# Two stages of each FFN's down-projection as seven products of quarters, with the weight sums made by accumulating DMAs

## The chip, the cores and the metric

The kernel runs on one core of one Trainium2 chip; the seven other cores are idle. The metric is the device time of one execution in microseconds, the median of three runs. TensorE (PE) multiplies, VectorE (DVE) and ScalarE (ACT) do the element-wise work, SyncE (SP) issues the loads, and GpSimd (POOL) sets a few small tiles.

## What is computed

Two layers on 512 tokens of 1024 features: in the first a retention mixer, in the second stick-breaking attention, each with a gated FFN behind it. The change is in the FFN:

```python
D_MODEL, SEQ, D_FF = 1024, 512, 2816
def _conv_ffn(h, w_up, conv_w, conv_b, w_down):
    u = h @ w_up                                  # [512, 2 * 2816]
    u = causal_depthwise_conv(u, conv_w) + conv_b # width 3
    gate, val = jnp.split(u, 2, axis=-1)
    return (jax.nn.silu(gate) * val) @ w_down     # [512, 2816] @ [2816, 1024]
x = x + _conv_ffn(_rmsnorm(x, g), ...)            # all in float32
```

## The kernel before

Activations lie feature-major, as tiles of 128 features by 512 tokens. The residual is eight such tiles, `self.x` (printed as x_72 to x_79 in the order of instructions). A float32 operand of a product is held as two float32r parts: `chunk` (L94) loads 128 x 1024 weights into a `raw` buffer (three of them, a DMA from SP, L101), ACT rounds them into `hi` (L102) and DVE takes the rest into `lo` (L103); there are four buffers of each. `split` (L79) does the same for activations. `mm3` (L106) makes each product of tiles out of three matmuls, hi by hi, hi by lo and lo by hi (L109 to L111).

`ffn` (L394) goes over 22 tiles f of the 2816 inner features. For each, `ffn_act` (L380) makes two up-projections of 24 matmuls (`up`, L367: scaling L374, convolution L375 and L377), the gate (L383, L384) and the split of the activation (L84, L85). `down` (L388) multiplies a stage of these tiles by its weights: layer 0 has stages of 8, 8 and 6 tiles, layer 1 stages of 8, 6 and 4, and its last four tiles belong to the final norm. The first two stages of a layer run in the middle of the loop over f, two tiles after the last one that they need. A stage goes over the eight output tiles m: one weight chunk of (k tiles x 128) columns, `proj` into one PSUM tile `att` (four buffers), and `add_to_x` (L160), one DVE addition of 512 columns to the residual (L161).

Every engine runs its own queue in order. A scheduler sets the order within each queue when the kernel is built; it puts the split of a chunk several chunks ahead of its matmuls, as far as the buffers reach.

Of the kernel before, what the change touches and what calls it, by code (L numbers as in the profile page):

```python
# [34 lines left out]
class Kernel:  # L35
    """Activations are kept feature-major ([128 features, 512 tokens] tiles), so every
    projection takes its operands as they lie. A float32 operand of a large product is held as
    hi + lo, each of 12 significant bits (float32r), and the product is hi*hi + lo*hi + hi*lo."""

    def __init__(self, ctx, tc, t):  # L40
# [20 lines left out]
    BUFS = {"xh": 8, "xl": 8, "qk": 8, "vv": 8, "yy": 16, "pp": 8, "tt": 8, "rr": 2, "cs": 4}  # L61

    def sb(self, tag, cols=S, dt=F32):
        return self.ap.tile([P, cols], dt, tag=tag, bufs=self.BUFS[tag], name=self.name(tag))

# [13 lines left out]
    def split(self, src, tag, cols=S, scale=None):  # L79
        """hi + lo = src (* scale, per partition), exactly."""  # L80
# [13 lines left out]
    def chunk(self, c, cols=CH):  # L94
        """Weight chunk c of the stream: [128, cols], as hi + lo."""
        nc = self.nc
        raw = self.raw()
        hi = self.wp.tile([P, CH], F32R, tag="hi", bufs=4, name=self.name("hi"))
        lo = self.wp.tile([P, CH], F32R, tag="lo", bufs=4, name=self.name("lo"))
        raw, hi, lo = raw[:, :cols], hi[:, :cols], lo[:, :cols]  # L100
        nc.sync.dma_start(raw, c)  # L101
# [4 lines left out]
    def mm3(self, out, a, b, start, stop):  # L106
        """out (+)= a.T @ b for a, b given as (hi, lo)."""
# [26 lines left out]
    def proj(self, w, xs, out=None):  # L134
        """Feature-major projection by one [nk x 128, 128] chunk of weights."""
# [11 lines left out]
    def out_proj_steps(self, name, base, ys, last):  # L147
        """XT += W.T @ y over the k tiles of ys; chunks hold [k tiles, 256 columns]."""
# [555 lines left out]
```

## Time and profile before

| | us |
|---|---|
| median of 3 runs | 1389.34 (1389.16 to 1389.47) |
| span of the profiled execution | 1387.6 |
| PE busy | 1375.7 (99%) |
| DVE busy | 940.1 (68%) |
| ACT busy | 592.6 (43%) |
| POOL busy | 6.8 (0%) |

The profiled execution is shown by its span, first to last instruction; the runs' time is 1.7 us more than it, and holds what lies before and after. Matmuls are pipelined, so a busy PE says only that some matmul was under way; how fast they follow each other is read from their starts. A group's line gives count, busy time, mean duration, and the idle time of its engine just before it with what ended that. A stretch of time (a window) gives busy time by engine and the granted TensorE clock, where 1.00 is 2.4 GHz and 0.50 is 1.2 GHz.

### The profile page before, as it was taken

How to read it: one execution, taken by the hardware profiler on the slowest of the kernel's cores; microseconds unless marked ns; L12 is line 12 of the kernel's file. 1: busy time of each engine (PE TensorE's matmuls, PEld its weight loads, DVE VectorE, ACT ScalarE, POOL GpSimd, SP SyncE). 2: the span in 40 equal slices, each digit the busy share in tenths (PEclk: the TensorE clock that was granted, in tenths of full speed). 3: DMA queues.
4: the chain of work that ended last, by engine and by line, in shares of the span. 5: the costliest groups of instructions: out<-in, count | busy, mean ns of one | idle time of the engine just before them, and what ended most of it. 6: DMA issues, size and time to landing. Idle time of an engine off the chain costs nothing.

```text
span 1387.6 us, 17028 instructions
## 1 busy us (share of the span) xinstructions
PE 1375.7 (99%) x6668; PEld 1140.9 (82%) x6668; DVE 940.1 (68%) x1282; ACT 592.6 (43%) x867; POOL 6.8 (0%) x69
## 2 busy tenths in 40 slices
PE   9999999999999999999999999999999999999997
PEld 7888888888888888888888888787788888888887
DVE  7774564654669773676367779889788753765765
ACT  5443332433355441443244655554355432433434
POOL 0000000000000000000000000000000000000000
PEclk9999999999999999999999999999999999999999
DMA  8233133131324333233322431120133233223221
GB/s 266 72 93 105 56 106 107 50 102 61 91 84 127 94 93 105 92 98 100 91 84 69 122 92 52 57 72 25 56 105 123 92 94 103 84 86 120 72 95 62
DMA packets 41025, 126.88 MB, mean 91 GB/s; under 512 B 4592, under 2 KB 6768, under 8 KB 40944
## 3 DMA queue, kind: packets, MB, share of 16 engines
q1 hardware_dynamic: 39424, 124.45, 29.0%
q10 hardware_dynamic: 1520, 1.33, 0.3%
q8 instruction: 53, 0.87, 0.3%
q14 instruction: 28, 0.23, 0.1%
HBM read 123.67 MB, written 2.10 MB: 91 GB/s over the span
## 4 chain that ended last, share of the span: by engine, by line
PE 96%; DVE 3%; ACT 0%; issue 0%; DMA 0%; DVEq 0%; ACTq 0%
PE acc L109 22%; PE acc L111 22%; PE acc L110 22%; PE att L109 8%; PE att L110 8%; PE att L111 8%; PE one L484 2%; PE z L458 1%; PE tp L476 1%; DVE cs L464 1%; DVE lo L103 1%; DVE tt L430 0%; DVE tt L427 0%; PE one L188 0%; PE one L223 0%
## 5 line engine op out<-in xcount | busy, mean ns | idle before, releaser
L102 ACT CAST hi<-raw 128x1024 fp32r<-128x1024 f32 (+2 forms) x253 | 244.6, 968 | 389.2 <-PE acc L110 182.0
L110 PE MATMUL acc<-xl,hi 128*128 128x512 f32 x960 | 374.6, 390 | 0.0
L111 PE MATMUL acc<-xh,lo 128*128 128x512 f32 x960 | 374.2, 390 | 0.0
L109 PE MATMUL acc<-xh,hi 128*128 128x512 f32 x960 | 374.2, 390 | 0.0
L103 DVE TENSOR_TENSOR lo<-raw,hi 128x1024 fp32r<-128x1024 f32 (+2 forms) x253 | 281.9, 1115 | 46.6 <-ACT hi L102 38.0
L111 PEld LDWEIGHTS acc<-xh,lo 128*128 128x128 f32 x960 | 180.2, 188 | 38.0 <-issue 0.5
L109 PEld LDWEIGHTS acc<-xh,hi 128*128 128x128 f32 x960 | 180.2, 188 | 36.6 <-issue 0.5
L110 PEld LDWEIGHTS acc<-xl,hi 128*128 128x128 f32 x960 | 180.3, 188 | 36.0
L377 DVE SCALAR_TENSOR_TENSOR tt<-tt,vec,tt 128x511 f32<-128x511 f32 (+1 forms) x176 | 131.2, 747 | 4.0 <-ACT tt L375 1.1
L374 DVE TENSOR_TENSOR tt<-acc,rr 128x512 f32<-128x512 f32 x80 | 55.0, 687 | 85.5 <-PE acc L111 85.5
L161 DVE TENSOR_TENSOR x<-x,att 128x512 f32<-128x512 f32 x40 | 27.4, 686 | 91.8 <-PE att L111 91.8
L109 PE MATMUL acc<-yy,hi 128*128 128x512 f32 x224 | 87.7, 392 | 0.1
L110 PE MATMUL acc<-yy,hi 128*128 128x512 f32 x224 | 87.6, 391 | 0.0
L111 PE MATMUL acc<-yy,lo 128*128 128x512 f32 x224 | 87.5, 391 | 0.0
L111 PE MATMUL acc<-hi,xl 128*128 128x512 f32 (+1 forms) x256 | 86.0, 336 | 0.0
L110 PE MATMUL acc<-lo,xh 128*128 128x512 f32 (+1 forms) x256 | 85.9, 336 | 0.0
L109 PE MATMUL acc<-hi,xh 128*128 128x512 f32 (+1 forms) x256 | 85.9, 336 | 0.0
L375 ACT ACTIVATE tt<-tt,vec 128x512 f32<-128x512 f32 x88 | 71.6, 814 | 7.5 <-DVE tt L374 6.4
L161 DVE TENSOR_TENSOR x<-x,acc 128x512 f32<-128x512 f32 x64 | 43.3, 684 | 43.2 <-PE acc L111 43.0
L111 PE MATMUL att<-yy,lo 128*128 128x512 f32 (+1 forms) x176 | 65.1, 370 | 0.0
L109 PE MATMUL att<-yy,hi 128*128 128x512 f32 (+1 forms) x176 | 65.1, 370 | 0.0
L110 PE MATMUL att<-yy,hi 128*128 128x512 f32 (+1 forms) x176 | 65.1, 370 | 0.0
(162 smaller groups left out, 1958.6 us busy)
## 6 DMA issues: line engine op xcount, KB each, us to landing
raw<-in_up SPq DMA_DIRECT2D x80, 512.0 KB, 3.6
raw<-in_down SPq DMA_DIRECT2D x24, 512.0 KB, 3.6
raw<-in_rv SPq DMA_DIRECT2D x16, 512.0 KB, 3.9
raw<-in_rg SPq DMA_DIRECT2D x16, 512.0 KB, 3.7
raw<-in_rout SPq DMA_DIRECT2D x16, 512.0 KB, 3.6
raw<-in_rqk SPq DMA_DIRECT2D x12, 512.0 KB, 3.7
raw<-in_down SPq DMA_DIRECT2D x16, 384.0 KB, 3.0
raw<-in_sqk SPq DMA_DIRECT2D x12, 512.0 KB, 3.7
```

The lines of the kernel that those rows point to most:

```text
L102: nc.scalar.copy(hi, raw)
L103: nc.vector.tensor_sub(lo, raw, hi.bitcast(F32))
L109: mm(out, a[0], b[0], start=start, stop=False)
L110: mm(out, a[0], b[1], start=False, stop=False)
L111: mm(out, a[1], b[0], start=False, stop=stop)
L161: self.nc.vector.tensor_add(self.x[m], self.x[m], ps)
L374: nc.vector.tensor_mul(u, ps, self.r)
L375: nc.scalar.activation(c, u, AF.Identity, scale=w[2], bias=w[3])
L377: nc.vector.scalar_tensor_tensor(c[:, i:], u[:, : S - i], w[2 - i], c[:, i:], op0=ALU.mult, op1=ALU.add)
L458: nc.tensor.matmul(z[:, :nz], q[:, i * P : (i + 1) * P], k[:, :nz], start=m == 0, stop=m == 1)
L464: nc.vector.tensor_tensor_scan(left[:, :n][:, ::-1], sg[:, :n][:, ::-1], self.diag[:, S - n :][:, ::-1], 0.0, op0=ALU.mult, op1=ALU.max,)
L484: self.nc.tensor.matmul(o[e * DH : (e + 1) * DH, i * P : (i + 1) * P], v[p // 4 * NT + j][:, h * DH : (h + 1) * DH], aT[e][:, j * P : (j + ...
```

## The change

For the first two stages of each FFN (`FAST`), the product of weights and activations is taken as 2 x 2 blocks: even and odd k tiles, even and odd output tiles, first and second 256 tokens. Seven products of blocks, with sums and differences as operands, take the place of eight.

- **Activations.** Two tiles f are collected in one tile `ar` of 2048 columns. DVE forms the differences T3, T1 (one operation of 512 columns), T2 and T4 (256 each), and one split of 1792 columns holds all seven operands (`oh`, `ol`).
- **Weights.** A stage runs as two halves of four output tiles (`fast_down`). A half loads w21, w11, w12 and w22 plainly (SP) and makes four sums by DMAs from POOL that add into the tile: w22 onto w21 in `sums`, then w11, then w12 onto the same tile, and w21 onto w11 in `raw`. Each sum is split by ACT and DVE before the next one is added. `sums` has two buffers, `hi` and `lo` now have five.
- **Products.** In order: T1 into z, X11 into x, T2 onto x, X21 into y (an `acc` tile), T3 onto x, X22 onto z, T4 onto x. Each goes over two output tiles p, 3 x (k tiles / 2) matmuls of 256 columns for each, and is followed by two additions of 256 columns to the residual. x and z go on accumulating after they have been read.
- **Memory.** Some activation buffers live in a pool per phase (`phase`), so that FFN and mixers share the space; the third stage uses `acc` tiles.

```diff
+FAST = (2, 2)
+Q = S // 2
...
+    def phase(self, which):
+        if self.pp is not None:
+            self.pp.__exit__(None, None, None)
+            self.pp = None
+        if which:
+            self.pp = self.tc.tile_pool(name=self.name(which), bufs=1, reuse_waits="tile")
+            self.ph = self.pp.__enter__()
...
-    BUFS = {"xh": 8, "xl": 8, "qk": 8, "vv": 8, "yy": 16, "pp": 8, "tt": 8, "rr": 2, "cs": 4}
+    BUFS = {"xh": 8, "xl": 8, "tt": 8, "rr": 2}
+    PHASE = {"qk": 8, "vv": 8, "yy": 16, "pp": 8, "cs": 4, "ar": 2, "oh": 5, "ol": 5}
...
         raw = self.raw()
-        hi = self.wp.tile([P, CH], F32R, tag="hi", bufs=4, name=self.name("hi"))
-        lo = self.wp.tile([P, CH], F32R, tag="lo", bufs=4, name=self.name("lo"))
+        nc.sync.dma_start(raw[:, :cols], c)
+        return self.parts(raw, cols)
+    def parts(self, raw, cols=CH):
+        nc = self.nc
+        hi = self.wp.tile([P, CH], F32R, tag="hi", bufs=5, name=self.name("hi"))
+        lo = self.wp.tile([P, CH], F32R, tag="lo", bufs=5, name=self.name("lo"))
         raw, hi, lo = raw[:, :cols], hi[:, :cols], lo[:, :cols]
-        nc.sync.dma_start(raw, c)
         nc.scalar.copy(hi, raw)
...
+    T3, T1, T2, T4, X21, X22, X11 = range(7)
     def ffn_act(self, l, f, ps):
         nc = self.nc
         g, v = self.up(l, f, ps[0]), self.up(l, NF + f, ps[1])
         nc.scalar.activation(g, g, AF.Silu)
-        nc.vector.tensor_mul(v, g, v)
-        tag = ("yy", "yy", "vv", "qk")[f % 4]
-        return self.split(v, (tag, tag))
+        if f % 2 == 0:
+            self.pair = self.sb("ar", 8 * Q)
+        y = self.pair[:, 6 * Q :] if f % 2 == 0 else self.pair[:, 4 * Q : 6 * Q]
+        nc.vector.tensor_mul(y, g, v)
+        if f >= STAGES[l][FAST[l] - 1][1]:
+            if f % 2 == 0:
+                self.two = self.sb("oh", 7 * Q, F32R), self.sb("ol", 7 * Q, F32R)
+            hi, lo = [x[:, f % 2 * S : (f % 2 + 1) * S] for x in self.two]
+            nc.scalar.copy(hi, y)
+            nc.vector.tensor_sub(lo, y, hi.bitcast(F32))
+            return hi, lo
+        if f % 2 == 0:
+            return None
+        part = lambda i, n=1: self.pair[:, i * Q : (i + n) * Q]
+        two = lambda x: x.rearrange("p (a q) -> p a q", a=2)
+        x12 = part(7)
+        nc.vector.tensor_sub(two(part(self.T3, 2)), two(part(self.X22, 2)), x12[:, None].broadcast_to([P, 2, Q]))
+        nc.vector.scalar_tensor_tensor(part(self.T2), part(self.T1), -1.0, part(self.X22), op0=ALU.mult, op1=ALU.subtract)
+        nc.vector.scalar_tensor_tensor(part(self.T4), part(self.T2), -1.0, part(self.X21), op0=ALU.mult, op1=ALU.subtract)
+        hi, lo = self.sb("oh", 7 * Q, F32R), self.sb("ol", 7 * Q, F32R)
+        nc.scalar.copy(hi, part(0, 7))
+        nc.vector.tensor_sub(lo, part(0, 7), hi.bitcast(F32))
+        return hi, lo
     def down(self, l, a, s, last):
         lo, hi = STAGES[l][s]
         for m in range(KD):
             w = self.wchunk(f"down{l}_{s}", m, (hi - lo) * P)
-            self.add_to_x(m, self.proj(w, a[lo:hi], None if last is not None else self.att()), last)
+            self.add_to_x(m, self.proj(w, a[lo:hi]), last)
+    def quarter(self, out, w, p, ops, n, start):
+        mm, nk = self.nc.tensor.matmul, len(ops)
+        for k, op in enumerate(ops):
+            c, o = slice((nk * p + k) * P, (nk * p + k + 1) * P), slice(n * Q, (n + 1) * Q)
+            a, b = [x[:, c] for x in w], [x[:, o] for x in op]
+            for i, (ai, bi) in enumerate(((0, 0), (0, 1), (1, 0))):
+                mm(out[:, :Q], a[ai], b[bi], start=start and k + i == 0, stop=k == nk - 1 and i == 2,
+                   skip_group_check=not start)
+    def fast_down(self, l, s, ops, half):
+        nc, t = self.nc, self.t[f"fast{l}_{s}"][half]
+        cols = 2 * len(ops) * P
+        w11, w12, w21, w22 = t[0], t[1], t[2], t[3]
+        first, second = slice(0, Q), slice(Q, S)
+        x = [self.psum("x", 2) for _ in range(2)]
+        z = [self.psum("z", 2) for _ in range(2)]
+        sums = self.wp.tile([P, CH], F32, tag="sums", bufs=2, name=self.name("sums"))
+        raw = self.raw()
+        def load(to, w, add=False):
+            if add:
+                nc.gpsimd.dma_start(to[:, :cols], w, accum_op=ALU.add)
+            else:
+                nc.sync.dma_start(to[:, :cols], w)
+        def product(to, w, n, start=False):
+            for p in range(2):
+                self.quarter(to[p], w, p, ops, n, start)
+        def add(row, tokens, of, sign=1):
+            for p in range(2):
+                x = self.x[4 * half + 2 * p + row][:, tokens]
+                (nc.vector.tensor_add if sign > 0 else nc.vector.tensor_sub)(x, x, of[p][:, :Q])
+        load(sums, w21)
+        load(sums, w22, True)
+        load(raw, w11)
+        w = self.parts(sums, cols)
+        product(z, w, self.T1, True)
+        add(1, second, z, -1)
+        load(sums, w11, True)
+        w = self.parts(raw, cols)
+        product(x, w, self.X11, True)
+        add(0, first, x)
+        load(raw, w21, True)
+        w = self.parts(sums, cols)
+        product(x, w, self.T2)
+        add(0, second, x)
+        load(sums, w12, True)
+        w = self.chunk(w12, cols)
+        y = [self.acc() for _ in range(2)]
+        product(y, w, self.X21, True)
+        add(0, first, y)
+        w = self.parts(raw, cols)
+        product(x, w, self.T3)
+        add(1, second, x, -1)
+        w = self.parts(sums, cols)
+        product(z, w, self.X22)
+        add(0, second, z)
+        w = self.chunk(w22, cols)
+        product(x, w, self.T4)
+        add(1, first, x, -1)
     def ffn(self, l, last):
         a, s = [], 0
         first = self.first4(f"ufirst{l}")
+        self.phase("ffn")
         for f in range(NF):
             a.append(self.ffn_act(l, f, first[2 * f : 2 * f + 2] if f < 2 else (None, None)))
+            if f == 1:
+                self.swap_pool()
             if s < 2 and f == STAGES[l][s][1] + 1:
-                self.down(l, a, s, None)
+                lo, hi = STAGES[l][s]
+                for half in range(2):
+                    self.fast_down(l, s, a[lo + 1 : hi : 2], half)
                 s += 1
+        self.swap_pool()
         self.down(l, a, s, last)
+        self.phase("mix" if last is not None else None)
         return a
...
+def _quarters(w, nk):
+    w = w.reshape(nk, 2, P, 2, 2, 2, P)
+    return w.transpose(3, 5, 1, 2, 4, 0, 6).reshape(2, 4, P, 2 * nk * P)
...
-            a[f"down{l}_{s}"] = _rows(ffn_w_down[l][lo * P : hi * P], hi - lo, P)
+            w = ffn_w_down[l][lo * P : hi * P]
+            if s < FAST[l]:
+                a[f"fast{l}_{s}"] = _quarters(w, (hi - lo) // 2)
+            else:
+                a[f"down{l}_{s}"] = _rows(w, hi - lo, P)
...
-    nc = _bacc.Bacc("TRN2", target_bir_lowering=False, num_devices=1)
+    nc = _bacc.Bacc("TRN2", target_bir_lowering=False, num_devices=1, dynamic_dma_scratch_size=1024)
```

What the change does to the queues, first on DVE in layer 0's first stage. Before, splits of weights (lo) and additions to the residual take turns; att is the PSUM tile of one output tile:

```order
L161 TENSOR_TENSOR x_74<-x_74,att_4028 128x512
L103 TENSOR_TENSOR lo_4152<-raw_4150,hi_4151 128x1024
L161 TENSOR_TENSOR x_75<-x_75,att_4060 128x512
L103 TENSOR_TENSOR lo_4184<-raw_4182,hi_4183 128x1024
L161 TENSOR_TENSOR x_76<-x_76,att_4092 128x512
L103 TENSOR_TENSOR lo_4216<-raw_4214,hi_4215 128x1024
L161 TENSOR_TENSOR x_77<-x_77,att_4124 128x512
L103 TENSOR_TENSOR lo_4253<-raw_4251,hi_4252 128x1024
```

After, the second half of the same stage: z, x and acc are PSUM tiles of 256 columns, x_75 to x_82 now the residual, sums_4201 and raw_4202 the two weight tiles that DMAs add into. The rows begin with the additions of the sixth product:

```order
L480 TENSOR_TENSOR x_77<-x_77,z_3972 128x256
L130 TENSOR_TENSOR lo_4269<-sums_4201,hi_4268 128x1024
L480 TENSOR_TENSOR x_76<-x_76,x_3969 128x256
L130 TENSOR_TENSOR lo_4302<-raw_4299,hi_4301 128x1024
L480 TENSOR_TENSOR x_78<-x_78,x_3970 128x256
L130 TENSOR_TENSOR lo_4334<-raw_4202,hi_4333 128x1024
L480 TENSOR_TENSOR x_80<-x_80,z_4199 128x256
L480 TENSOR_TENSOR x_82<-x_82,z_4200 128x256
L130 TENSOR_TENSOR lo_4364<-sums_4201,hi_4363 128x1024
L480 TENSOR_TENSOR x_79<-x_79,x_4197 128x256
L480 TENSOR_TENSOR x_81<-x_81,x_4198 128x256
```

The split of the sums for product 13 (lo_4364) now stands ahead of the additions of product 9 (x_79 and x_81 from x), and that for product 10 (lo_4269) behind the additions of product 6.

On POOL, before, the queue goes from its set-up straight to the small tiles of the attention (cs):

```order
L225 ISA
L225 AFFINE_SELECT diag<-diag 128x128
L463 MEMSET cs_6034 128x1
L463 MEMSET cs_6082 128x1
L463 MEMSET cs_6125 128x1
```

After, 32 DMAs stand there; these are the nine of layer 0's first stage and of the next stage's first sum (sums_5068):

```order
L469 DMA sums_3973<-in_fast_0 128x1024
L469 DMA sums_4201<-in_fast_0 128x1024
L469 DMA sums_3973<-in_fast_0 128x1024
L469 DMA raw_3974<-in_fast_0 128x1024
L469 DMA sums_3973<-in_fast_0 128x1024
L469 DMA sums_5068<-in_fast_1 128x1024
L469 DMA sums_4201<-in_fast_0 128x1024
L469 DMA raw_4202<-in_fast_0 128x1024
L469 DMA sums_4201<-in_fast_0 128x1024
```

A DMA into sums_4201 stands behind the first one of the next stage, and the three into it follow one another.

At the same stage's start, on DVE, before (tt, yy: the last activation and its split; att_3964: the stage's first output tile):

```order
L377 SCALAR_TENSOR_TENSOR tt_3947<-tt_3946,vec,tt_3947 128x511
L377 SCALAR_TENSOR_TENSOR tt_3947<-tt_3946,vec,tt_3947 128x510
L384 TENSOR_TENSOR tt_3947<-tt_3910,tt_3947 128x512
L85 TENSOR_TENSOR yy_3955<-tt_3947,yy_3954 128x512
L161 TENSOR_TENSOR x_72<-x_72,att_3964 128x512
L103 TENSOR_TENSOR lo_4088<-raw_4086,hi_4087 128x1024
L161 TENSOR_TENSOR x_73<-x_73,att_3996 128x512
L103 TENSOR_TENSOR lo_4120<-raw_4118,hi_4119 128x1024
```

After, where ar is the pair of activations and z and x are the tiles of products 1 to 3 of the first half:

```order
L404 SCALAR_TENSOR_TENSOR tt_3955<-tt_3954,vec,tt_3955 128x510
L480 TENSOR_TENSOR x_78<-x_78,z_3972 128x256
L418 TENSOR_TENSOR ar_3884<-tt_3918,tt_3955 128x512
L480 TENSOR_TENSOR x_75<-x_75,x_3969 128x256
L431 TENSOR_TENSOR ar_3884<-ar_3884 128x512
L130 TENSOR_TENSOR lo_4136<-sums_3973,hi_4135 128x1024
L432 SCALAR_TENSOR_TENSOR ar_3884<-ar_3884 128x256
L480 TENSOR_TENSOR x_77<-x_77,x_3970 128x256
L433 SCALAR_TENSOR_TENSOR ar_3884<-ar_3884 128x256
L480 TENSOR_TENSOR x_75<-x_75,x_3969 128x256
L130 TENSOR_TENSOR lo_4168<-raw_4165,hi_4167 128x1024
```

The additions of products 1 to 3 now stand among the last activations' differences (ar) and the split for product 6 (lo_4136).

## Rows read from the trace of the kernel before

**Rows 1.** The page: busy time by engine, and the chain that ended last.

```profile
PE 1375.7 (99%) x6668; PEld 1140.9 (82%) x6668; DVE 940.1 (68%) x1282; ACT 592.6 (43%) x867; POOL 6.8 (0%) x69
PE 96%; DVE 3%; ACT 0%; issue 0%; DMA 0%; DVEq 0%; ACTq 0%
```

**Rows 2.** Stretches (columns in the first line): the four stages, then an up-projection.

```profile
core 0: us, PE busy (x) PEld busy (x) DVE busy (x) ACT busy (x) POOL busy (x), PEclk, DMA share, GB/s
511.20:554.70 43.50, 43.50 (x193) 36.04 (x192) 18.00 (x20) 9.77 (x11) 0.00 (x0) 1.00 0.31 97
641.80:685.30 43.50, 43.50 (x194) 36.02 (x193) 18.00 (x20) 9.76 (x11) 0.00 (x0) 1.00 0.32 97
1124.50:1168.00 43.50, 43.50 (x194) 36.03 (x192) 18.00 (x20) 9.77 (x11) 0.00 (x0) 1.00 0.31 98
1233.30:1265.90 32.60, 32.60 (x145) 27.02 (x144) 16.52 (x20) 8.68 (x11) 0.00 (x0) 1.00 0.38 110
446.00:489.50 43.50, 43.50 (x194) 36.02 (x193) 31.75 (x40) 19.67 (x26) 0.00 (x0) 1.00 0.32 98
```

**Rows 3.** PE in time: start us, length us, engine, line, operation.

```profile
1339.58 0.39 PE L110 MATMUL att<-vv,hi 128*128 128x512 f32 x1
...
1352.73 0.39 PE L111 MATMUL att<-yy,lo 128*128 128x512 f32 x1
1352.96 0.28 PE L109 MATMUL att<-vv,hi 128*128 128x256 f32 x1
...
1364.47 0.28 PE L109 MATMUL att<-vv,hi 128*128 128x256 f32 x1
```

**Rows 4.** Groups by shape on DVE: count, then busy us, mean ns, idle before.

```profile
L103 DVE TENSOR_TENSOR lo<-raw,hi 128x1024 fp32r<-128x1024 f32 x193 | 235.6, 1221 | 31.3 <-ACT hi L102 26.7 <-PE att L110 1.5
L377 DVE SCALAR_TENSOR_TENSOR tt<-tt,vec,tt 128x511 f32<-128x511 f32 x88 | 65.6, 745 | 1.3 <-ACT tt L375 1.1
L103 DVE TENSOR_TENSOR lo<-raw,hi 128x512 fp32r<-128x512 f32 x40 | 27.3, 685 | 15.4 <-ACT hi L102 11.3 <-PE one L188 4.1
L103 DVE TENSOR_TENSOR lo<-raw,hi 128x768 fp32r<-128x768 f32 x20 | 19.1, 954 | 0.0
L568 DVE TENSOR_TENSOR x<-x,att 128x256 f32<-128x256 f32 x16 | 6.7, 417 | 6.1 <-PE att L111 5.6
```

**Rows 5.** Groups by shape on ACT: the splits' first halves.

```profile
L102 ACT CAST hi<-raw 128x1024 fp32r<-128x1024 f32 x193 | 203.2, 1053 | 319.6 <-PE acc L110 157.8 <-PE att L110 121.6 <-issue 17.5
L102 ACT CAST hi<-raw 128x768 fp32r<-128x768 f32 x20 | 16.8, 839 | 24.7 <-PE acc L110 10.7 <-PE att L110 9.2 <-ACT pp L461 2.8
```

**Rows 6.** DVE and ACT in time, at the first stage's start.

```profile
511.18 1.05 ACT L102 CAST hi<-raw 128x1024 fp32r<-128x1024 f32 x1 [0.95 <-PE acc L110]
...
512.26 1.23 DVE L103 TENSOR_TENSOR lo<-raw,hi 128x1024 fp32r<-128x1024 f32 x1 [0.17 <-ACT hi L102]
```

**Rows 7.** All of POOL's work in the loop: the one group that repeats.

```profile
L463 POOL MEMSET cs<- 128x1 f32 x64 | 6.3, 98 | 975.5 <-DVE pp L468 646.0 <-DVE pp L291 278.4 <-DVE tt L236 50.7
```

**Rows 8.** DMA issues: count, KB each, us from issue to landing.

```profile
raw<-in_down SPq DMA_DIRECT2D x24, 512.0 KB, 3.6
raw<-in_down SPq DMA_DIRECT2D x16, 384.0 KB, 3.0
raw<-in_down SPq DMA_DIRECT2D x8, 256.0 KB, 2.6
```

**Rows 9.** SP's issue of the weights: duration ns, lowest, median and highest.

```profile
L101 SPq DMA_DIRECT2D raw<-in_down x48: 327/328/328, 480.9 to 1336.3; - x48
```

**Rows 10.** Stretches after the last matmul; PEclk is the granted clock.

```profile
1379.00:1380.00 1.00, 0.09 (x1) 0.00 (x0) 0.36 (x1) 0.47 (x1) 0.00 (x0) 1.00 0.00 0
1380.00:1381.00 1.00, 0.00 (x0) 0.00 (x0) 1.00 (x1) 0.00 (x0) 0.00 (x0) 1.00 0.00 0
1381.00:1382.00 1.00, 0.00 (x0) 0.00 (x0) 0.96 (x2) 0.00 (x0) 0.00 (x0) 0.77 0.00 0
1382.00:1384.00 2.00, 0.00 (x0) 0.00 (x0) 1.99 (x5) 0.00 (x0) 0.00 (x0) 0.50 0.44 147
```

More of the change, by code (lines that the diff above doesn't have):

```diff
@@ L46, in __init__ @@
         self.n = 0
+        self.pp = None
         self.att_pool()
+        self.phase("mix")
     def att_pool(self):
-        self.pa = self.tc.tile_pool(name=self.name("pa"), bufs=1, space=bass.MemoryType.PSUM)
+        self.pa = self.tc.tile_pool(name=self.name("pa"), bufs=1, space=bass.MemoryType.PSUM, reuse_waits="tile")
         self.pt = self.pa.__enter__()
+    def phase(self, which):
+        if self.pp is not None:
+            self.pp.__exit__(None, None, None)
+            self.pp = None
+        if which:
+            self.pp = self.tc.tile_pool(name=self.name(which), bufs=1, reuse_waits="tile")
+            self.ph = self.pp.__enter__()
     def swap_pool(self):
@@ L59, in name @@
         return f"{s}_{self.n}"
-    BUFS = {"xh": 8, "xl": 8, "qk": 8, "vv": 8, "yy": 16, "pp": 8, "tt": 8, "rr": 2, "cs": 4}
+    BUFS = {"xh": 8, "xl": 8, "tt": 8, "rr": 2}
+    PHASE = {"qk": 8, "vv": 8, "yy": 16, "pp": 8, "cs": 4, "ar": 2, "oh": 5, "ol": 5}
     def sb(self, tag, cols=S, dt=F32):
-        return self.ap.tile([P, cols], dt, tag=tag, bufs=self.BUFS[tag], name=self.name(tag))
+        pool, bufs = (self.ap, self.BUFS) if tag in self.BUFS else (self.ph, self.PHASE)
+        return pool.tile([P, cols], dt, tag=tag, bufs=bufs[tag], name=self.name(tag))
     def acc(self, cols=S):
```

## The prediction

> **What bounds the kernel now.** The page's totals come first: PE is busy for 99% of the span and the chain that ended last is 96% PE [rows 1]. A busy PE need not be a full one, so the second view is time by stretches: the four stretches that the change rewrites, the first two stages of the down-projection in each FFN, hold PE busy from end to end, 43.5 us for three of them and 32.6 us for the one with six k tiles, while DVE works 18.0 us of 43.5 and POOL nothing [rows 2]. The third view is PE's own order of starts. 58 starts of 512 columns lie between 1339.58 and 1352.73, 0.2267 us apart, and 96 starts of 256 columns between 1352.96 and 1364.47, 0.1199 us apart [rows 3]. So two matmuls of 256 columns take 0.2398 us, 6% more than one of 512: each start costs 0.013 us that has nothing to do with its columns. PE sets the time here, and a stage gets shorter only by what its own matmuls get shorter and longer by every wait that reaches PE.
>
> **What is removed and added on PE.** A stage of 8 k tiles has 8 output tiles x 8 x 3 = 192 matmuls of 512 columns: 192 x 0.2267 = 43.5 us, the stretch in [rows 2]. After, it has 14 products (two halves of seven) of 24 matmuls of 256 columns: 336 x 0.1199 = 40.3 us. It gains 3.2 us, not the eighth (5.4 us) that the count of products suggests. The stage of 6 k tiles goes from 144 x 0.2267 = 32.6 to 252 x 0.1199 = 30.2, a gain of 2.4. Sum: 3 x 3.2 + 2.4 = **12.0 us**, the most that the change can bring: 1389.3 - 12.0 = 1377.3. The profiled execution spans 1387.6 us and the median of the runs is 1389.34, so 1.7 us lie outside the span and are left as they are.
>
> **What is added off PE, and hidden.** In the up-projections two activations now cost DVE a 512-wide and two 256-wide differences and one split of 1792 columns in place of two splits of 512. From 0.685 us for 512 and 1.221 for 1024 [rows 4], a column costs 1.05 ns, and 1792 make 2.02: 0.69 + 2 x 0.45 (between 0.42 for a 256-wide addition and 0.75 for a fused operation of 511) + 2.02 - 2 x 0.69 = +2.2 us for each 21.8 us of PE. DVE goes there from 31.75 to some 36.2 us of 43.5 [rows 2]. That still fits, so I cost it at nothing; without the cover it would be 2.2 us a pair. In a stage DVE goes to 14 splits of 1.22 and 28 additions of 0.42 [rows 4], 28.9 us of 40.3, and ACT to 14 x 1.05 = 14.7 [rows 5]. Both fit on average. The pools opened per phase reuse memory whose readers ended during the 21.8 us of the four first projections; nothing. The 32 further loads are no load on bandwidth, with a DMA share of 0.31 to 0.38 in these stages [rows 2].
>
> **What lands on the path.** Call a half's products 1 to 7 and 8 to 14; one takes 24 x 0.1199 = 2.88 us. The sums of weights are one tile that is split (ACT, then DVE), then changed in place by an accumulating DMA, then split again: for products 8, 10 and 13 in the second half. Split, DMA, split, DMA, split is a chain that PE doesn't pace. DVE's order makes it bind earlier than at product 13: the split for product 13 stands ahead of the addition of product 9, and product 10 accumulates on the tile that this addition reads, so PE can't start product 10 before the second DMA has landed.
>
> Let L be the time of one accumulating DMA from the end of the split to its landing. In the first stage, from the end of product 4: 0.16 us until its last matmul is out (0.28 long, 0.12 apart, [rows 3]), its second addition 0.42, split 1.22, L, ACT 1.05 and DVE 1.22, L, 1.05 and 1.22 again, addition 0.42, and some six hand-overs taken at 0.1 each (from ACT's end at 512.23 to DVE's start at 512.26 it is 0.03, [rows 6]; those to and from a DMA no row shows). That is 7.3 + 2L, against five products, 14.4 us, in which PE would get there: **wait = 2L - 7.1**. Layer 1's first stage has the same order. In layer 0's second stage the split for product 8 stands ahead of product 4's additions and waits only for the buffer of product 3: 8.0 + 2L against six products, 17.3: 2L - 9.3. In the stage of 6 k tiles a product takes 2.16, ACT 0.84 and DVE 0.95 for 768 columns [rows 4, 5]: 7.2 + 2L' against 13.0: 2L' - 5.8. In the first halves the same chain starts some 10 us earlier, beside up-projections of 5.4 us each, and has room for any L up to about 10.
>
> Before has no accumulating DMA and no DMA from POOL, which sets 64 tiny tiles and is otherwise idle [rows 7]. Its price is bounded by plain loads: 2.6, 3.0 and 3.6 us for 256, 384 and 512 KB [rows 8], so 1.6 us whatever the size and 2.0 for 512 KB. The lower end is a plain load, 3.6: an accumulation does all that a load does, and reads its target too, so I exclude less. The upper end is two transfers one behind the other, 7.2. In between, with one fixed part and two readings, 1.6 + 2 x 2.0 = 5.6; a second list to issue at SP's 0.33 [rows 9] makes 5.9, and 4.7 for 384 KB. I take **L = 5.9 and 4.7**, since one DMA has one landing. The waits are 4.7 + 4.7 + 2.5 + 3.6 = **15.5 us**.
>
> A page states another price: the Trainium skill, DMA: Bandwidth & Descriptors, section "Anatomy of one DMA — SWDGE (gpsimd) path", fits a DMA issued from GpSimd as 2.0 us plus its bytes at 436 GB/s. No run here shows it; an estimate from that page with the bytes counted twice is 4.4 us for 512 KB and 3.8 for 384, waits of 1.7 + 1.7 + 0 + 1.8, and a sum of 1386.5.
>
> There is a second, smaller wait at a stage's start, where DVE still has the last activations. From the end of the last up-projection it works 0.69 + 1.22 + 0.75 + 0.42 + 0.75 + 0.42 + 0.69 + 0.42 = 5.4 us to the first addition of product 2, just in time for product 3 at 5.8; then 0.69 + 1.22 + 0.45 + 0.42 = 2.8 to the second, where PE has 2.0 us of other matmuls. 0.5 us by the rows, more with hand-overs: 1.0 a stage, **4.0 us**.
>
> And the clock: after the last matmul ended at 1379.1 the granted clock was 1.00 until 1381 and 0.50, the 1.2 GHz level, from 1382 on [rows 10]. Waits of 2.5 to 4.7 us are of that length. Columns that cost 0.1068 us for 256 at the full clock cost twice that at half, 2.6 us on a product; how soon the clock returns no row shows. Between 0 and 2.6 a wait I take half, 4 x 1.3 = **5.2 us**.
>
> Sum: -12.0 + 15.5 + 4.0 + 5.2 = +12.7, so 1389.3 + 12.7 = **1402 us**. With L = 5.6 and no clock loss it is 1389.3 - 12.0 + 13.1 + 4.0 = 1394; with 7.2 and 6.0 and the whole clock loss 1389.3 - 12.0 + 25.9 + 4.0 + 10.4 = 1418.
>
> **Rivals.** *The DMA is as quick as a plain load and the change pays.* Speaking for it: the queue is empty and the DMA share is a third [rows 2]. At L = 3.6 and 3.0 the waits are 0.1 + 0.1 + 0 + 0.2, the start waits 4.0 at most: 1389.3 - 12.0 + 4.4 = 1382, and 1377 with nothing left. Against it: it reads twice, and POOL issues it. It decides the other way from L of about 4.9 on, where waits of 2.7 + 2.7 + 0.5 + 2.0 and the 4.0 eat the 12.0. *Break-even*: L of 4.3 to 5.0 and the clock untouched, 1387 to 1392. *POOL is held up*: DVE's splits fall between the steps by which POOL prepares its list, one or two of 1.22 us for each DMA: L = 8.3 and 7.1, waits of 9.5 + 9.5 + 7.3 + 8.4 = 34.7, clock 10.4, together 1426. Against it: DVE is idle for a third of a stage, and before shows nothing of the kind. The Trainium skill, SBUF — State Buffer, section "SBUF: two separate sides", has such a rule: a DMA issued from GpSimd starves while DVE holds the port pair that both share, in its two-port modes. No run here shows it, and the page limits it for operations with two inputs, as the splits are, to GpSimd work that reads SBUF.
>
> **How the numbers follow.** 0.2% of 1389 is 2.8 us, about what a measurement of this kernel can tell from no change. Forecast (L from 5 to 7.5, 1393 to 1420): 0.58. Held up further, above 1420: 0.12. Break-even: 0.17. Pays: 0.13. Slower 0.70, same 0.17, faster 0.13. The range leaves out the lower half of "pays" and the upper part of "held up": 1384 to 1424.
>
> **What would show it.** A steady 0.12 us between the starts of the 256-column matmuls shows the gain term. PE's waits before L452 at product 10 of each stage, released by DVE's addition L480, itself behind a split L130 that waited for a DMA of POOL, show the chain; their sizes over two give L. Two short waits before product 3 show the start term, and a granted clock under 1.0 in slices of the four stages shows the last one. If PE has no wait at product 10, the prediction is wrong, and so it is if the 256-column starts lie further apart than 0.12 or DVE falls behind in the up-projections.

## The result, and the profile after

The changed kernel takes 1404.39 us (median of 4 runs, 1401.99 to 1404.72) against 1389.25 for the kernel before: a ratio of 1.0104, 95% interval 1.009 to 1.0118. It is slower by 15 us at the median and by 12.6 us in span in the profiled execution (1400.2 against 1387.6), which was the quickest of the four. The forecast was 1402.

First the page of the changed kernel: busy time by engine, and the chain that ended last.

```profile
PE 1371.3 (98%) x7208; PEld 1163.2 (83%) x7208; DVE 1012.9 (72%) x1416; ACT 618.4 (44%) x876; POOL 34.8 (2%) x101
PE 84%; issue 7%; DVE 4%; DMA 3%; ACT 1%; POOL 0%; DVEq 0%; ACTq 0%; POOLq 0%
```

Its DMA issues: count, KB each, us from issue to landing.

```profile
sums<-in_fast POOLq DMA_DIRECT2D x18, 512.0 KB, 5.5
raw<-in_fast SPq DMA_DIRECT2D x18, 512.0 KB, 3.6
...
raw<-in_fast POOLq DMA_DIRECT2D x6, 512.0 KB, 6.4
...
sums<-in_fast POOLq DMA_DIRECT2D x6, 384.0 KB, 5.0
```

Against [rows 1] PE is still busy for 98%, so the totals hardly tell that anything is wrong; the chain does, in which PE fell from 96% to 84% and DVE and DMA have a share. It tells where to look, not how much is lost: 12% of the span are 168 us, and the loss is 12.6 (issue is time that the profile puts to no wait). An accumulating DMA lands 5.5 us after its issue where a plain load of the same size takes 3.6, as in [rows 8].

Next the four stages of the changed kernel and the up-projection of [rows 2], as stretches.

```profile
core 0: us, PE busy (x) PEld busy (x) DVE busy (x) ACT busy (x) POOL busy (x), PEclk, DMA share, GB/s
512.00:558.80 46.80, 42.09 (x338) 41.89 (x337) 32.01 (x49) 16.80 (x16) 4.36 (x5) 0.96 0.68 169
645.80:691.00 45.20, 42.26 (x338) 41.88 (x338) 29.76 (x46) 15.91 (x16) 4.43 (x6) 0.96 0.68 174
1130.60:1177.00 46.40, 41.77 (x338) 41.59 (x337) 32.10 (x49) 16.77 (x16) 4.36 (x5) 0.96 0.64 159
1242.30:1278.40 36.10, 31.91 (x253) 31.70 (x252) 25.77 (x45) 13.66 (x16) 2.62 (x3) 0.95 0.51 129
447.00:490.50 43.50, 43.50 (x194) 36.02 (x193) 36.32 (x46) 20.49 (x24) 0.00 (x0) 1.00 0.37 109
```

From their first start of 256 columns to the next start of 512, the stages take 46.8, 45.2, 46.4 and 36.1 us: 174.5 in all, where 720 starts of [rows 3] made 163.2. The stages hold 11.3 of the 12.6 us. The other 1.3 lie outside them; what they are stays open. PE is idle in each stage, and its clock is below 1.00.

Where PE is idle, its own rows say: the changed kernel's PE in time, with the idle time and its releaser in brackets.

```profile
537.82 0.28 PE L452 MATMUL x<-oh,lo 128*128 128x256 f32 x1
542.80 0.49 PE L452 MATMUL x<-oh,hi 128*128 128x256 f32 x1 [4.71 <-DVE x L480]
...
665.86 0.28 PE L452 MATMUL x<-oh,lo 128*128 128x256 f32 x1
668.30 0.35 PE L452 MATMUL z<-oh,hi 128*128 128x256 f32 x1 [2.17 <-DVE x L480]
...
676.54 0.35 PE L452 MATMUL x<-oh,hi 128*128 128x256 f32 x1 [0.77 <-DVE x L480]
...
1161.30 0.55 PE L452 MATMUL x<-oh,hi 128*128 128x256 f32 x1 [4.63 <-DVE x L480]
...
1266.59 0.58 PE L452 MATMUL x<-oh,hi 128*128 128x256 f32 x1 [4.19 <-DVE x L480]
```

Measured from start to start less the usual 0.12, the lost times are 4.86, 2.32 and 0.93, 4.78 and 4.35: **17.2 us**. All but the second stand before product 10, all are released by an addition L480, and no other gap in the stages is as long as 0.15 us, but for the first step behind a long wait. The second, 2.32, stands before product 8, whose tile z the forecast had not looked at.

What the addition waited for is in the rows of DVE, ACT and POOL in the second half of layer 0's first stage.

```profile
524.39 1.22 DVE L130 TENSOR_TENSOR lo<-sums,hi 128x1024 fp32r<-128x1024 f32 x1
...
525.97 0.87 POOL L469 DMA_DIRECT2D sums<-in_fast  x1 [1.89 <-DVE x L480]
...
531.62 1.05 ACT L129 CAST hi<-sums 128x1024 fp32r<-128x1024 f32 x1 [6.95 <-DMA sums<-in_fast]
...
532.70 1.22 DVE L130 TENSOR_TENSOR lo<-sums,hi 128x1024 fp32r<-128x1024 f32 x1 [2.78 <-ACT hi L129]
...
534.33 0.88 POOL L469 DMA_DIRECT2D sums<-in_fast  x1 [5.95 <-DVE x L480]
...
540.03 1.04 ACT L129 CAST hi<-sums 128x1024 fp32r<-128x1024 f32 x1 [4.64 <-DMA sums<-in_fast]
541.11 1.22 DVE L130 TENSOR_TENSOR lo<-sums,hi 128x1024 fp32r<-128x1024 f32 x1 [3.59 <-ACT hi L129]
542.25 0.75 DVE L480 TENSOR_TENSOR x<-x,x 128x256 f32<-128x256 f32 x2
```

This is the chain that was forecast: split for product 8, DMA, split for 10, DMA, split for 13, and only then, at 542.25, the two additions of product 9, whose last matmul was out at 538.1. PE goes on at 542.80. L, from the end of a split to the ACT step on the new bytes, is 525.61 to 531.62, 6.0 us, and 533.92 to 540.03, 6.1.

Last the clock behind the first of these waits: PE's clock is the column before the DMA share.

```profile
537.00:540.00 3.00, 1.10 (x10) 0.89 (x8) 0.52 (x2) 0.00 (x0) 0.00 (x0) 1.00 0.98 259
...
542.80:546.00 3.20, 3.19 (x15) 3.20 (x16) 1.64 (x3) 0.00 (x0) 0.00 (x0) 0.51 0.73 182
546.00:547.00 1.00, 1.00 (x9) 1.00 (x8) 0.10 (x1) 0.00 (x0) 0.34 (x1) 0.86 0.81 238
```

For 3.2 us after the wait the granted clock is 0.51, the 1.2 GHz level, and 15 matmuls start where 26 would. Stage length less the same stage without any wait (40.31, 40.30, 40.32 and 30.24 in the last kernel of the experiments) less the wait leaves 1.6, 1.6, 1.3 and 1.6: **6.1 us** for the clock.

### The profile page after: what moved, and what is told of

The parts are those of the page before. It is cut to its first block, busy times and chain, and to the rows that moved or that the text cites. A ratio compares the mean times of both kernels' runs of the same rounds, so it can differ in the third digit from the quotient of the medians.

```text
span 1400.2 us, 18420 instructions
## 1 busy us (share of the span) xinstructions
PE 1371.3 (98%) x7208; PEld 1163.2 (83%) x7208; DVE 1012.9 (72%) x1416; ACT 618.4 (44%) x876; POOL 34.8 (2%) x101
## 4 chain that ended last, share of the span: by engine, by line
PE 84%; issue 7%; DVE 4%; DMA 3%; ACT 1%; POOL 0%; DVEq 0%; ACTq 0%; POOLq 0%
PE acc L136 21%; PE acc L138 21%; PE acc L137 21%; PE x L452 4%; PE att L136 3%; PE att L137 3%; PE att L138 3%; DMA sums<-in_fast 3%; PE z L452 2%; PE one L608 2%; PE z L582 1%; PE tp L600 1%; PE acc L452 1%; DVE lo L130 1%; ACT hi L129 1%
## 5 line engine op out<-in xcount | busy, mean ns | idle before, releaser
L188 DVE TENSOR_TENSOR x<-x,acc 128x512 f32<-128x512 f32 x72 | 48.9, 685 | 50.6 <-PE acc L138 50.4
L452 PE MATMUL x<-oh,hi 128*128 128x256 f32 x240 | 70.4, 293 | 14.3 <-DVE x L480 14.3
L136 PE MATMUL acc<-yy,hi 128*128 128x512 f32 x192 | 75.1, 391 | 0.0
L138 PE MATMUL acc<-yy,lo 128*128 128x512 f32 x192 | 75.1, 391 | 0.0
L137 PE MATMUL acc<-yy,hi 128*128 128x512 f32 x192 | 75.0, 391 | 0.0
L452 PE MATMUL x<-ol,hi 128*128 128x256 f32 x240 | 69.8, 291 | 0.0
L452 PE MATMUL x<-oh,lo 128*128 128x256 f32 x240 | 69.7, 290 | 0.0
L452 PEld LDWEIGHTS x<-oh,hi 128*128 128x128 f32 x240 | 48.1, 200 | 15.0 <-ACT hi L129 9.7
```

The lines of the kernel that those rows point to most:

```text
L136: mm(out, a[0], b[0], start=start, stop=False)
L137: mm(out, a[0], b[1], start=False, stop=False)
L138: mm(out, a[1], b[0], start=False, stop=stop)
L188: self.nc.vector.tensor_add(self.x[m], self.x[m], ps)
L452: mm(out[:, :Q], a[ai], b[bi], start=start and k + i == 0, stop=k == nk - 1 and i == 2, skip_group_check=not start)
```

## The experiments

All times below are medians, beside runs of the kernel before on the same chip (1389.7 to 1389.8 us).

| run | what differs from the changed kernel | us | ratio to before |
|---|---|---|---|
| e1_own_loads | no sums, each quarter by its own load | 1378.11 | 0.9917 (0.9902 to 0.9932) |
| e2_sync_in_place | SP writes in place of POOL's adding | 1380.85 | 0.994 (0.9925 to 0.9954) |
| e3_pool_plain | POOL writes in place of adding | 1386.72 | 0.9975 (0.9966 to 0.9985) |
| e4_dve_sums | the chain's two sums on DVE | 1381.38 | 0.9939 (0.9924 to 0.9954) |
| e5_order | split for product 13 later on DVE | 1385.18 | 0.997 (0.9961 to 0.998) |
| e6_fill | PE works in three of the waits | 1401.93 | 1.0088 (1.0073 to 1.0103) |
| e7_dve_order | sums on DVE, and splits later | 1378.03 | 0.9916 (0.9901 to 0.9931) |
| e8_order_all | all DMAs kept, three splits later | 1379.5 | 0.9925 (0.9912 to 0.9937) |
| e9_again | nothing | 1405.41 | 1.0111 (1.0095 to 1.0126) |

**Is the chain the whole loss?** The first kernel takes it away.

```
-        load(sums, w21)
-        load(sums, w22, True)
-        load(raw, w11)
-        w = self.parts(sums, cols)
+        w = self.chunk(w21, cols)
...
-        load(sums, w11, True)
-        w = self.parts(raw, cols)
+        w = self.chunk(w11, cols)
```

> Each of the seven products of a half takes one plain quarter of the weights by a load of its own from SP; the sums of weights are left out, so the output is another. The chain of two accumulating DMAs is gone, the 1260 matmuls of 256 columns, the splits and the additions stay. Theory (the chain and the clock behind it are the whole loss): no wait of PE over 0.3 us in the four stages, stages of 40.3 and 30.2 us, granted clock 1.00 in them, 1389.3 - 12.0 + 1.3 (what the changed kernel was longer outside its four stages) = 1378.6, between 1377 and 1381. Rival 1 (the order of splits ahead of additions on DVE costs the waits by itself, whatever feeds the splits): waits of 2 us or more stay before product 10, 1388 or more. Rival 2 (the 256-column products are dearer in company than the 0.1199 us a start): no waits but stages over 42 us, 1384 or more.

Its stages, first layer 0's first and then layer 1's second, as stretches:

```profile
512.10:552.50 40.40, 40.40 (x337) 40.36 (x337) 32.37 (x49) 16.99 (x16) 0.00 (x0) 1.00 0.59 169
...
1225.30:1255.60 30.30, 30.30 (x253) 30.25 (x252) 25.75 (x45) 13.83 (x16) 0.00 (x0) 1.00 0.64 181
```

1378.11 us. PE is busy from end to end, at clock 1.00, with the same 336 matmuls, 14 splits and 28 additions. So 256-column products cost what [rows 3] said, DVE has room in the stages, and the waits and the clock behind them go with the sums. A split of weights still stands ahead of product 9's additions on DVE (536.34 ahead of 537.48), so this order alone costs PE nothing. Both rivals fall.

**Is it the length of the DMA?** Two kernels change only how the later quarters come into their tiles.

```
-                nc.gpsimd.dma_start(to[:, :cols], w, accum_op=ALU.add)
+                nc.sync.dma_start(to[:, :cols], w)
```

> The accumulating DMAs from POOL become plain loads from SP into the same tiles, with the same waits on the splits; the sums are left out, so the output is another. Theory (wait = 2L less a constant, L the time from a split's end to the ACT step on the new bytes, 6.1 us in the changed kernel for 512 KB): L = 0.3 issue + 3.6 landing + 0.4 hand-over = 4.2, 1.9 less, so each wait falls by 3.8: from 4.9, 3.3, 4.8 and 4.4 to 1.1, 0, 1.0 and 0.6; with some 1 us of clock 1389.3 - 12.0 + 1.3 + 2.7 + 1 = 1382, between 1379 and 1386. Rival (the length of the DMA isn't what counts; the chain is held by the hand-overs or by DVE): waits of 4 us stay, 1398 or more. Second rival: SP stands waiting for the split, the weights of the up-projections behind it come late and PE waits there: over 1390 with new waits outside product 10.

1380.85 us, as the theory said: the waits before product 10 are 1.15, 0.22, 0.22 and 0.69, the clock stays at 1.00, and no new wait shows. Both rivals fall.

```
-                nc.gpsimd.dma_start(to[:, :cols], w, accum_op=ALU.add)
+                nc.gpsimd.dma_start(to[:, :cols], w)
```

> The accumulating DMAs stay on POOL, in the same order, but write instead of adding; the sums are left out, so the output is another. It tells POOL's issue from the second reading. Theory as the prediction sized L (1.6 fixed, 2.0 for each reading of 512 KB, 0.33 for issue): one reading less, L = 6.1 - 2.0 = 4.1, waits as in the run with SP, 1382 (1379 to 1386). Rival (the issue on POOL is the dear part, 0.87 us of it in the trace, and adding costs little): L falls by less than 0.7, waits by less than 1.4 each, 1395 or more. The DMA page's price for a DMA issued from GpSimd (2.0 us and the bytes at 436 GB/s) would be 3.2 to landing.

The second of them, plain writes from POOL, in the same place as the chain above: the ends of both DMAs and PE behind them.

```profile
525.97 0.53 POOL L469 DMA_DIRECT2D sums<-in_fast  x1 [2.36 <-DVE lo L130]
530.60 1.05 ACT L129 CAST hi<-sums 128x1024 fp32r<-128x1024 f32 x1 [5.87 <-DMA sums<-in_fast]
...
533.30 0.53 POOL L469 DMA_DIRECT2D sums<-in_fast  x1 [5.22 <-DVE x L480]
...
537.40 1.05 ACT L129 CAST hi<-sums 128x1024 fp32r<-128x1024 f32 x1 [3.86 <-DMA sums<-in_fast]
...
537.88 0.28 PE L452 MATMUL x<-oh,lo 128*128 128x256 f32 x1
540.18 0.55 PE L452 MATMUL x<-oh,hi 128*128 128x256 f32 x1 [2.03 <-DVE x L480]
```

And its DMAs from POOL:

```profile
sums<-in_fast POOLq DMA_DIRECT2D x18, 512.0 KB, 4.0
```

Without the adding, POOL's step is 0.53 us in place of 0.87 and the landing 4.0 in place of 5.5; from SP it is 3.7. The time with POOL's plain writes, 1386.7, misses the expected 1379 to 1386 and lies between the theory (1382) and its rival (1395): without the adding L falls by 1.1 and 1.6 us, not 2.0. The next table has the wait before product 10 in layer 0's first stage, from start to start less 0.12, against the two L of its chain, in five traces.

| trace | L, first and second | their sum less 7.25 | wait |
|---|---|---|---|
| e2_sync_in_place | 4.54, 3.84 | 1.13 | 1.15 |
| e3_pool_plain | 4.93, 4.50 | 2.18 | 2.18 |
| changed kernel | 6.01, 6.11 | 4.87 | 4.86 |
| e9_again | 6.54, 6.52 | 5.81 | 5.83 |
| e6_fill | 5.85, 8.75 | 7.35 | 7.36 |

One constant, 7.25, fits all within 0.03 us. The forecast had 2L - 7.1. Every us on a DMA of this chain is a us of waiting for PE.

**Why do the runs differ?** A second look at the changed kernel, without any edit:

> The changed kernel itself once more, for a second profile: its runs went from 1402.0 to 1404.7 and the profiled one was the quickest. Theory: the wait at product 10 of layer 0's first stage is the two DMA times of its chain (split's end to the next ACT step) less 7.25 us, as in the four traces at hand, 12.1 - 7.25 = 4.9, 9.4 - 7.25 = 2.2, 8.4 - 7.25 = 1.1, 14.6 - 7.25 = 7.4; here too within 0.2 us, and the time is longer by what the DMAs are. Rival: the two DMA times and the wait go apart by over 0.5 us, and the runs differ for another reason.

The wait follows L as expected: 6.5 in place of 6.1 made it 5.83. The time, 1405.41 us, does not follow the DMAs alone. Of the 3.4 us between the two profiled executions of the changed kernel, longer waits are 1.5 (18.7 us for 17.2) and the clock is 1.8 (7.9 for 6.1, reckoned as above). Behind the wait in layer 1's first stage it was at half speed for over 5 us, in place of 2.8 (1161.3 to 1164.1):

```profile
1162.50:1168.00 5.50, 5.48 (x26) 5.50 (x27) 1.76 (x3) 0.20 (x1) 0.86 (x1) 0.50 0.69 177
```

L varies from run to run, and in one trace from 5.85 to 8.75 between two DMAs of one chain. Why one of them took 8.75 stays open. One repeated case has a visible neighbour: in layer 0's second stage the first L is 8.4 and 8.2 in the two traces of the changed kernel, and 9.4 in e6_fill, where POOL had issued another accumulating DMA, the next stage's, about 1 us ahead. That this neighbour is the cause was not tried. It fits that the DMA of 512 KB into raw, 1.5 to 2.6 us behind one of the chain, lands in 6.7 to 8.8 us in the second halves of the changed kernel, and in 5.4 to 5.6 where DVE makes the chain's sums (e4_dve_sums) and the chain's DMAs are gone. The DMA with the L of 8.75 had no such neighbour. The `dynamic_dma_scratch_size=1024` of the diff, which all these kernels share, was not varied.

**Can DVE make the sums?** w11 and w12 are loaded for other products of the half anyway.

```
-        load(sums, w11, True)
+        nc.vector.tensor_add(sums[:, :cols], sums[:, :cols], raw[:, :cols])
...
-        load(sums, w12, True)
-        w = self.chunk(w12, cols)
+        r12 = self.raw()
+        load(r12, w12)
+        nc.vector.tensor_add(sums[:, :cols], sums[:, :cols], r12[:, :cols])
+        w = self.parts(r12, cols)
```

> In each half two of the four accumulating DMAs, the two of the chain, become additions of 1024 columns on DVE (768 in the last stage), from tiles that are loaded for other products anyway; all sums are formed, as in the changed kernel. Theory: a step of the chain falls from 6.1 us to some 1.3, and what is left is the single DMA of the other sum, whose split also stands ahead of product 9's addition: 15.3 against 14.4 us, a wait of 0 to 1.5 in each stage; DVE goes to some 34 of 40.3 us. 1389.3 - 12.0 + 1.3 + 2 (0 to 6) = 1381, between 1379 and 1386, quicker than both kernels. Rival (DVE has no room for it at a stage's start or beside the up-projections): new waits behind DVE before products 3 to 7, 1388 or more.

1381.38 us, with waits before product 10 of 0.78, none, 0.93 and 1.40 us, as expected: the one DMA left behind a split on DVE is still just too late.

**Is it the DMA, or who stands behind it?** These two keep every accumulating DMA and move splits on DVE, by a copy of one column that a later split overwrites.

```
+        if after is not None:
+            nc.vector.tensor_copy(lo[:, :1], after)
         nc.vector.tensor_sub(lo, raw, hi.bitcast(F32))
...
-        w = self.parts(sums, cols)
+        w = self.parts(sums, cols, self.x[4 * half + 2][:, Q : Q + 1] if half else None)
         product(z, w, self.X22)
```

> The changed kernel with its four accumulating DMAs a half, and one thing moved: in the second halves a copy of one column makes the split for product 13 stand behind the addition of product 10 on DVE instead of ahead of product 9's. Nothing is left out. Theory (the chain reaches PE early only through DVE's order; the chain itself ends some 0.4 + 1.4 + 2 x 6.1 + 2 x 2.3 = 18.6 us after product 4, and PE comes to product 13 after eight products, 23.0 us): no wait at product 10 and none at 13, in the stage of 6 k tiles 17.3 against some 17.5, a wait under 1; granted clock 1.00; 1389.3 - 12.0 + 1.3 + 0.5 = 1379, between 1377 and 1382. Rival (the sums themselves come too late for PE, and the order only decides where it shows): the waits go to product 12 or 13 with 2 us or more each, 1388 or more.

The expected 1379 was missed: 1385.18 us, 1381.6 to 1388.3 between runs. The profiled execution is the quickest of the ten, so its waits are less than the usual ones. The wait before product 10 of layer 0's first stage fell from 4.86 to 0.18, but others stayed, 2.07, 0.76 and 0.45. The longest, in layer 0's second stage, on DVE and then on PE:

```profile
659.36 1.22 DVE L132 TENSOR_TENSOR lo<-sums,hi 128x1024 fp32r<-128x1024 f32 x1 [5.51 <-ACT hi L129]
660.50 0.74 DVE L482 TENSOR_TENSOR x<-x,z 128x256 f32<-128x256 f32 x2
...
658.87 0.28 PE L454 MATMUL x<-oh,lo 128*128 128x256 f32 x1
661.06 0.35 PE L454 MATMUL z<-oh,hi 128*128 128x256 f32 x1 [1.92 <-DVE x L482]
```

DVE stands 5.5 us before the split for product 10, and behind it are the additions of product 6, which must read z before product 8 may overwrite it. That explains the wait before product 8 in the changed kernel too. In layer 1's first stage the split for product 12, which waits for the DMA into raw, stood ahead of product 9's additions in the same way. The next kernel moves all three splits.

```
+        w = self.parts(sums, cols, self.x[2][:, Q : Q + 1] if half else None)
         product(x, w, self.T2)
...
+        w = self.parts(raw, cols, self.x[4 * half][:, Q : Q + 1] if half else None)
         product(x, w, self.T3)
```

> The changed kernel with all its accumulating DMAs, nothing left out, and three splits moved on DVE in the second halves: for product 10 behind the addition of product 6, for products 12 and 13 behind the addition of product 10. The run that moved the split for product 13 alone still waited 2.1 us in layer 0's second stage, where the addition of product 6 stood behind the split for product 10, and its time went from 1381.6 to 1388.3 between runs. Theory (the DMAs cost PE nothing as long as no addition that PE needs stands behind a split that waits for one; the spread is that of L, 5.9 to 8.8 us in the traces): no wait over 0.3 us at product 8, 10, 12 or 13, 1378.3 (1377 to 1381), and runs within 1.5 us of each other. Rival (an accumulating DMA is late for PE by itself in some runs): 1381 to 1388 with a spread of several us, waits at product 10 or 13 released by its own split L132.

1379.5 us, 1378.3 to 1380.45. Its stages took 40.31, 40.37, 40.32 and 30.88 us, with one wait of 0.54, in the 6-k-tile stage, at the third matmul of product 13 and for its own split:

```profile
1251.81 0.39 PE L454 MATMUL z<-oh,lo 128*128 128x256 f32 x1 [0.38 <-DVE lo L132]
```

That is the kind of wait that the rival names, at a fraction of its size. It is over the expected 0.3, and order has a part in it again: ACT took these sums at 1247.67, when they had landed, and the weights for product 12 behind them; so the split for product 12 and behind it the one for 13, at 1250.80, were late on DVE. The spread, 2.2 us, is a little over the 1.5 expected, and a third of that of the kernel before it. So the accumulating DMAs, with L of 6 us and more, cost little by themselves, 1.4 us against the kernel without sums; what cost 23 us was that additions, which PE needed, were queued behind splits that waited for them.

The splits moved and the sums on DVE together:

> The kernel whose two sums of the chain are formed by DVE, and with it the splits for products 12 and 13 put behind the addition of product 10 on DVE. Nothing is left out. Theory: the waits of 0.8, 0.9 and 1.4 us that were left before product 10 go, 1381.4 - 3.1 = 1378.3 (1377 to 1380), the floor that the kernel with loads of its own showed (1378.1). Rival (the last accumulating DMA is late for product 12 in the 6-k-tile stage): 1 to 2 us stay there, 1380.

```profile
511.50:551.80 40.30, 40.30 (x337) 40.28 (x336) 32.65 (x51) 16.66 (x16) 2.63 (x3) 1.00 0.57 148
...
1224.50:1254.70 30.20, 30.20 (x253) 30.20 (x252) 26.21 (x48) 12.68 (x15) 0.87 (x1) 1.00 0.42 110
```

1378.03 us (1377.81 to 1378.72), the quickest kernel that forms all sums, 11.7 us ahead of the kernel before: the floor of the one without sums.

**Does the clock fall because PE is idle?** Here PE works for 4.2 us of the wait, before product 10 in three of the stages.

```
+        if half and (l, s) != (0, 1):
+            fill = self.acc()
+            for i in range(34):
+                nc.tensor.matmul(fill[:, :Q], w[0][:, :P], ops[0][0][:, :Q], start=i == 0, stop=i == 33)
         w = self.parts(sums, cols)
         product(x, w, self.T2)
```

> The changed kernel with 34 matmuls of 256 columns (4.1 us) into a spare tile right ahead of product 10, in the second halves of the three stages that wait 4.4 to 4.9 us there; nothing reads them. PE then works in the wait. Theory (the half clock behind the wait comes from PE's idleness): product 10 starts when it did, at full clock; the 14 to 16 starts 0.213 apart go back to 0.120, 1.4 + 1.6 + 1.7 us with the slow first one: 1404.4 - 4.7 = 1399.7, between 1398 and 1402. Rival (the clock falls for another reason, or the longer matmuls are PE waiting for weights): the half rate stays, 1403 to 1406.

PE in layer 1's first stage:

```profile
1160.46 4.24 PE L496 MATMUL acc<-oh,hi 128*128 128x256 f32 x34
1165.30 0.36 PE L452 MATMUL x<-oh,hi 128*128 128x256 f32 x1 [0.60 <-DVE x L480]
```

Stretches behind that wait, and behind the one in layer 0's first stage:

```profile
1165.00:1167.00 2.00, 1.70 (x14) 1.73 (x15) 1.67 (x3) 0.79 (x1) 0.00 (x0) 1.00 0.53 167
...
546.00:548.00 2.00, 2.00 (x14) 2.00 (x14) 1.02 (x2) 0.00 (x0) 0.00 (x0) 0.69 0.76 262
```

1401.93 us, inside the expected range but above its middle. Where the fill left 0.76 and 1.21 us idle, in layer 1, the clock stayed at 1.00. In layer 0's first stage L was 8.75, PE was idle for 3.3 us behind the fill, and the clock fell. So in each stage the clock followed PE's idleness; the theory holds, though the gain was 2.5 us beside the first runs of the changed kernel (3.5 beside the second) and not 4.7.

## Why the prediction was right, point by point

**The gain**, -12.0 us, was right: the starts of 256 columns lie 0.12 apart, and without waits the stages take 40.3 and 30.2 us, to 0.1. The best kernel gained 11.7.

**The hidden work** was right. DVE has 36.32 us in the up-projection's 43.5, forecast some 36.2, and PE works through; a kernel with all of it and no waits reaches the floor.

**The chain** was right as a mechanism, 17.2 us where 15.5 stood. The wait at product 10, its releaser and its slope were as forecast. Three sizes were off. L of 512 KB was 6.0 and 6.1 for 5.9. For 384 KB it was 5.4 and 5.6 for 4.7, which with a constant of 6.7 in place of 5.8 made 4.35 for 3.6. In layer 0's second stage one L was 8.4, and most of the wait came before product 8, by way of z, which the working had overlooked: 3.25 for 2.5. The chain's formula holds there all the same. Without waits product 10 would start 216 x 0.1199 = 25.9 us into the stage, at 671.74; it starts at 676.54, 4.8 late, which is 2L less 9.6 where the forecast had 9.3. The second look (4.7) and e6_fill (6.3) give 9.6 too. PE shows 3.25 of the 4.8 as waits and spends the rest on slow matmuls of products 8 and 9, so the half clock cost this stage nothing beyond the chain.

The 5.9 was built as 1.6 + 2 x 2.0 + 0.33. Measured, the adding costs 1.5 in the landing, 0.34 of it in POOL's step, and a DMA from POOL 0.3 over one from SP; whether the rest of the 1.5 is the second reading, no run tells.

The Trainium skill, DMA: Bandwidth & Descriptors, section "Anatomy of one DMA — SWDGE (gpsimd) path", has 2.0 us and the bytes at 436 GB/s, an estimate of 3.2 for a plain 512 KB. Here that landed in 4.0, and in 5.5 with adding, where the estimate from the page was 4.4; its sum of 1386.5 was too low.

**The start wait**, 4.0 us, was the step that failed: it is none. DVE's rows at the stage's start show why.

```profile
512.23 0.69 DVE L401 TENSOR_TENSOR tt<-acc,rr 128x512 f32<-128x512 f32 x1 [1.91 <-PE acc L138]
...
515.22 0.74 DVE L404 SCALAR_TENSOR_TENSOR tt<-tt,vec,tt 128x510 f32<-128x510 f32 x1
515.88 0.41 DVE L480 TENSOR_TENSOR x<-x,z 128x256 f32<-128x256 f32 x1
516.21 0.68 DVE L418 TENSOR_TENSOR ar<-tt,tt 128x512 f32<-128x512 f32 x1
516.81 0.41 DVE L480 TENSOR_TENSOR x<-x,x 128x256 f32<-128x256 f32 x1
...
519.22 0.41 DVE L480 TENSOR_TENSOR x<-x,x 128x256 f32<-128x256 f32 x1
```

Instructions that don't wait start 0.08 us before the one ahead ends: 0.41 long, 0.33 apart. I had added lengths. They make 8.1 us from 512.23 to the end of product 2's second addition; measured it is 7.4, at 519.63, and PE comes to the matmuls that need it at 519.82. The 0.7 too much is more than the wait of 0.5 that the rows had given (0.4 by its own terms). The other half of the 4.0 was taken for hand-overs, without a row.

**The clock**, 5.2 us between 0 and 10.4, came to 6.1: about 1.5 a wait, where half of the bound of 2.6 was taken. In the second look it came to 7.9, so 6.1 is one draw and not a constant.

**The sum**: -12.0 + 17.2 + 0 + 6.1, and 1.3 outside the stages, make 12.6 in the profiled execution. That the forecast's +12.7 is the same number is luck in part: the start wait, 4.0 too high, was made up by the chain (1.7 more), the clock (0.9) and the 1.3 outside the stages, and the profiled execution was the quickest. The medians differ by 15.1.

**The rivals.** A DMA as quick as a plain load gave 1381 in the trial with SP, where the prediction said 1382. The two are so close by offsetting errors: with L of 4.5 and 3.8 in place of 3.6 PE waited for 2.3 us where 0.4 was forecast, and the start waits of 4.0 were none. POOL was not held up, as the durations of its DMA steps in the changed kernel show (lowest, median, highest, ns):

```profile
L469 POOL DMA_DIRECT2D sums<-in_fast x24: 865/865/1013, 34.6 to 1259.2; - x24
```

The step at 525.97 in the chain above took 0.87 us while DVE ran a split from 525.86 on. No trace here shows the starving that the Trainium skill, SBUF — State Buffer, section "SBUF: two separate sides", warns of.

## What to carry to other kernels

When work is taken off the bounding engine, ask of each new wait what is queued behind it on the engine that waits: a slow DMA costs little (1.4 us here) until an instruction that the bounding engine needs stands behind its consumer. A chain that feeds back through one tile costs its latency once per link, so the same sums on a second path (1378.0 us), or a consumer placed later in the queue (1379.5), were worth more here than a quicker DMA (1380.9 with plain loads). And where a term is a small difference between two engines' schedules, take the distance between starts, not the sum of lengths.

## What the runs showed of the hardware that was not expected

- Half clock followed every wait of 2.2 us and more in these traces (2.18 with POOL's plain writes: 0.53 from 540 to 542), for 2.8 to 5.8 us of the work behind it. Why it held longer in some stages than in others stays open. Near 2 us the length did not decide: in layer 0's second stage a wait of 2.08 in the second look at the changed kernel was followed by 0.50 (671 to 673), one of 2.07 with one split moved by 1.00 throughout. Waits of 1.5 us and less left it at 1.00.
- Accumulating DMAs of one size spread widely: L from 5.85 to 8.75 us in one chain, and up to 9.4. A kernel in which PE waited behind them spread over 6.7 us between runs (one split moved), the one that forms the chain's sums on DVE and lets no split stand in the way over 0.9 us.
- For POOL, adding costs in the issue as well: 0.87 us a step in place of 0.53.
